# Rotary embedding on one core: cosine and sine tables loaded through ScalarE's queue instead of GpSimd's, and replicated without fill, shuffle or packing

## Chip, core and metric

One core of a Trainium2 chip. The metric is the device time of one execution in microseconds, the median of three runs. Engines are named as in the profile: DVE is VectorE, ACT is ScalarE, POOL is GpSimd, SP is SyncE; a trailing q means the engine's instruction queue. L96 is line 96 of the kernel before.

## What is computed

`x` has 16 batches of 512 positions with 16 heads of 64 floats. Half of each head is rotated, the other half passes through. The tables `cos` and `sin` have 512 rows of 32 floats, of which only the first 16 are used.

```python
x1, x2 = x[..., :32], x[..., 32:]
c, s = cos[None, :, None, :16], sin[None, :, None, :16]
first  = x1[..., :16] * c - x1[..., 16:] * s
second = x1[..., :16] * s + x1[..., 16:] * c
out = concatenate([first, second, x2], -1)
```

The input of x and the output are 33.55 MB each; each table is 64 KB.

## The kernel before

The flattened input is cut into T = 4 tiles of 128 partitions; a partition holds K = 16 successive positions of 16 heads, 64 KB in one piece. A ring of NS = 3 tiles lies in SBUF. A tile is loaded whole, rotated in place and stored whole, the half x2 travelling along untouched.

Tile 2 is loaded in two halves, since only the first half is wanted early. SyncE's queue carries, in this order: load 0, load 1, the first half of load 2 (lines 65 to 67); then, behind a wait for the rotation of tile 0, store 0, the second half of load 2, and load 3 (which takes the ring slot of tile 0 and so waits for store 0 to have landed); then store 1 and store 3. Store 2 is issued from POOL's queue (line 116). A dependency put in by hand (lines 118 to 123) holds store 1 until the second piece of tile 2 has been rotated.

`rotate` (lines 90 to 103) does one piece of a tile on VectorE in four instructions: x1 times sine into a PSUM tile (L96), x1 times cosine in place (L97), a subtraction for the first quarter (L98) and an addition for the second (L101). The pieces are half tiles, except that the second half of tile 2 is cut in 5 and 3 positions.

Because 512 positions are 32 partitions of 16, partition p of every tile needs table row p modulo 32. The lines before the first rotation build `table`, which holds for all 128 partitions and 16 positions the 16 cosines twice and the 16 sines twice, so that one multiply covers both quarters:

- L61: VectorE fills the first quarters of `stage` with zeros.
- L62 to 64: POOL's queue loads the 32 rows of each table (2 KB a row) to every fourth partition of `stage`, one transfer for the cosines and one for the sines. Both wait for L61.
- L73: a shuffle within each group of 32 partitions brings the eight filled rows of that group to the right places of `spun`.
- L80: four copies, of 32, 24, 16 and 8 partitions, put the rows of the four groups together on partitions 0 to 31 (`packed`).
- L83: four copies of 32 partitions and 1024 elements write `packed` to the four groups of `table`, doubling each row by reading it twice.

The order of work is that of the program text on each engine's queue; semaphores are placed by the tile framework from the data dependencies.

Of the kernel before, what the change touches and what calls it, by code (L numbers as in the profile page):

```python
# [1 line left out]

# [4 lines left out]


@with_exitstack
def kernel(  # L10
    ctx: ExitStack,
    tc: tile.TileContext,
    x: bass.AP,
    cos: bass.AP,
    sin: bass.AP,
    out: bass.AP,
):
    nc = tc.nc
    fp32 = mybir.dt.float32
    P = 128  # L20
    B, S, H, D = x.shape
    Q = D // 4
    HF = D // 2

    K = 16
    T = B * S // (P * K)
    PB = S // K
    REP = P // PB  # L30
    R = H * D
    NS = 3
    KC = K // 2
    KM = 13

    xf = x.rearrange("b s h d -> (b s h d)").rearrange("(t p f) -> t p f", t=T, p=P)
    of = out.rearrange("b s h d -> (b s h d)").rearrange("(t p f) -> t p f", t=T, p=P)
    cosf = cos.rearrange("(p k) j -> p (k j)", k=K)
    sinf = sin.rearrange("(p k) j -> p (k j)", k=K)

    const_pool = ctx.enter_context(tc.tile_pool(name="const", bufs=1))
    b_pool = ctx.enter_context(tc.tile_pool(name="bp", bufs=1, space=bass.MemoryType.PSUM))


    ring = const_pool.tile([P, NS, K, H, D], fp32)
    stage = const_pool.tile([P, 2, K, HF], fp32)
    spun = const_pool.tile([P, 2 * K, Q], fp32)
    packed = const_pool.tile([PB, 2 * K, Q], fp32)
    table = const_pool.tile([P, 2, K, 2, Q], fp32)

    def rows(t, lo, hi):
        return ring[:, t % NS, lo:hi].rearrange("p k h d -> p (k h d)")

    def load(t, lo=0, hi=K):
        return nc.sync.dma_start(out=rows(t, lo, hi), in_=xf[t, :, lo * R : hi * R])

    def store(t, lo=0, hi=K, queue=nc.sync):
        return queue.dma_start(out=of[t, :, lo * R : hi * R], in_=rows(t, lo, hi))  # L58


    nc.vector.memset(stage[:, :, :, 0:Q], 0.0)  # L61
    spread = stage.rearrange("(j b) t k i -> j b t (k i)", b=REP)  # L62
    nc.gpsimd.dma_start(out=spread[:, 0, 0], in_=cosf)  # L63
    nc.gpsimd.dma_start(out=spread[:, 0, 1], in_=sinf)  # L64
    load(0)
    load(1)
    load(2, 0, KC)

    PQ = PB // REP
    nc.vector.stream_shuffle(  # L73
        out=spun[:],
        in_=stage.rearrange("p t k j -> p (t k) j")[:, :, 0:Q],
        mask=[j % PQ * REP for j in range(PB)],
    )
    for q in reversed(range(REP)):
        n = PQ * (q + 1)
        nc.vector.tensor_copy(out=packed[0:n], in_=spun[q * PB : q * PB + n])  # L80

    for r in range(REP):
        nc.vector.tensor_copy(  # L83
            out=table[r * PB : (r + 1) * PB].rearrange("p t k c j -> p (t k) c j"),
            in_=packed.unsqueeze(2).to_broadcast((PB, 2 * K, 2, Q)),
        )
    C = table[:, 0].rearrange("p k c j -> p k (c j)")
    Sn = table[:, 1].rearrange("p k c j -> p k (c j)")

    def rotate(t, lo, hi):  # L90
        x1 = ring[:, t % NS, lo:hi, :, 0:HF]
        c = C[:, lo:hi].unsqueeze(2).to_broadcast((P, hi - lo, H, HF))
        s = Sn[:, lo:hi].unsqueeze(2).to_broadcast((P, hi - lo, H, HF))
        b_full = b_pool.tile([P, KC, H, HF], fp32, name="b_t")
        b_t = b_full[:, 0 : hi - lo]
        nc.vector.tensor_mul(out=b_t, in0=x1, in1=s)  # L96
        nc.vector.tensor_mul(out=x1, in0=x1, in1=c)  # L97
        nc.vector.tensor_sub(  # L98
            out=x1[:, :, :, 0:Q], in0=x1[:, :, :, 0:Q], in1=b_t[:, :, :, Q:HF]
        )  # L100
        return nc.vector.tensor_add(  # L101
            out=x1[:, :, :, Q:HF], in0=x1[:, :, :, Q:HF], in1=b_t[:, :, :, 0:Q]
        )

    rotate(0, 0, KC)
    rotate(0, KC, K)
    store(0)
    load(2, KC, K)
    load(3)
    rotate(1, 0, KC)  # L110
    rotate(1, KC, K)
    behind_loads = store(1)
    rotate(2, 0, KC)
    near = rotate(2, KC, KM)
    rotate(2, KM, K)
    store(2, queue=nc.gpsimd)

    tc.add_manual_dep(
        behind_loads.ins,
        near.ins.name,  # L120
        mybir.DependencyInfo(mybir.DependencyClass.Sync, mybir.DependencyReason.DATA),
        reason="the store follows the loads at the DMA engines",
    )
    rotate(3, 0, KC)
    rotate(3, KC, K)
    store(3)


# [1 line left out]
_INS = ['x', 'cos', 'sin']  # L130
_OUTS = [((16, 512, 16, 64), 'float32')]


# [23 lines left out]
```

## Time and profile before

| | |
|---|---|
| three runs | 161.46, 161.57, 162.91 us; median 161.57 |
| profiled execution | span from first to last instruction 159.5 us; its own time outside the profiler is not given |
| VectorE busy | 112.9 us (71% of the span), 47 instructions |
| POOL busy | 1.9 us, 7 instructions |
| ScalarE, TensorE | no work |
| bytes moved | 67.24 MB, 422 GB/s over the span |
| HBM read, written | 33.69 MB, 33.55 MB |
| cosine transfer, issue to landing | 8.9 us |
| sine transfer, issue to landing | 13.3 us |
| VectorE's longest wait | 14.4 us, at the shuffle, for the sine transfer |

A profile row of section 5 of the page names line, engine, operation, tiles and shapes, then total busy time and the mean of one instruction, then the idle time ahead of it and what ended that. DMA shares are those of 16 transfer engines; the queue called q1 holds the transfers issued from SyncE, q0 those from POOL. "Packet records" in the text are the trace's single entries for each packet on each transfer engine, with start, duration and size.

### The profile page before, as it was taken

The page shows a single profiled execution, that of the slowest core. Times are in us where ns is not written, and L with a number is a line of the kernel's source. Part 1 is how long each engine was busy: PE and PEld are TensorE (multiplying, and loading weights), DVE is VectorE, ACT ScalarE, POOL GpSimd, SP SyncE. Part 2 cuts the span into 40 slices and gives each one's busy share as a digit, 9 for nine tenths or more (in the row PEclk, how much of TensorE's full clock was granted, in tenths as well). Part 3 has the DMA queues.
Part 4 walks back from the last instruction along what each step waited for, and adds up shares of the span by engine and source line. Part 5 has one row for each costly group of instructions (what it writes and reads, how often), then busy time and mean ns, then how long its engine had stood idle before and what let it go on. Part 6 is the DMA issues. An engine that isn't in the chain of part 4 may idle for free.

```text
span 159.5 us, 115 instructions
## 1 busy us (share of the span) xinstructions
DVE 112.9 (71%) x47; POOL 1.9 (1%) x7
## 2 busy tenths in 40 slices
DVE  1000959999999999999999999999999990000000
POOL 3000000000000000000000000010000000000000
DMA  7969979899699699699996996996996996998966
GB/s 263 542 263 542 444 345 526 362 427 526 271 493 551 263 526 526 263 395 427 493 526 263 526 526 263 526 526 263 526 526 263 526 510 279 526 427 362 526 263 263
DMA packets 1360, 67.24 MB, mean 422 GB/s; under 512 B 176, under 2 KB 176, under 8 KB 208
## 3 DMA queue, kind: packets, MB, share of 16 engines
q1 hardware_dynamic: 1152, 58.72, 85.7%
q0 software_dynamic: 208, 8.52, 12.4%
HBM read 33.69 MB, written 33.55 MB: 422 GB/s over the span
## 4 chain that ended last, share of the span: by engine, by line
DVE 61%; DMA 14%; issue 5%; DVEq 1%
DVE b_t L96 22%; DVE ring L97 22%; DMA ring<-in_x_dram 14%; DVE ring L101 10%; DVE ring L98 7%; DVEq L152 1%; DVEq L96 0%
## 5 line engine op out<-in xcount | busy, mean ns | idle before, releaser
L96 DVE TENSOR_TENSOR b_t<-ring,table 128x4096 f32<-128x4096 f32 (+2 forms) x9 | 35.6, 3959 | 2.1 <-DMA ring<-in_x_dram 1.9
L97 DVE TENSOR_TENSOR ring<-ring,table 128x4096 f32<-128x4096 f32 (+2 forms) x9 | 35.6, 3950 | 0.3
L98 DVE TENSOR_TENSOR ring<-ring,b_t 128x2048 f32<-128x2048 f32 (+2 forms) x9 | 18.4, 2050 | 0.3
L101 DVE TENSOR_TENSOR ring<-ring,b_t 128x2048 f32<-128x2048 f32 (+2 forms) x9 | 18.4, 2043 | 0.0
L73 DVE LOAD_MASK_SELECT spun<-stage x1 | 0.0, 14 | 14.4 <-DMA stage<-in_sin_dram 14.4
L83 DVE COPY table<-packed 32x1024 f32<-32x1024 f32 x4 | 2.7, 684 | 0.1
L58 POOL DMA_DIRECT2D out_dram<-ring x1 | 0.6, 559 | 101.7 <-DVE ring L101 101.7
L80 DVE COPY packed<-spun 32x512 f32<-32x512 f32 (+3 forms) x4 | 1.7, 416 | 0.1
L61 DVE MEMSET stage<- 128x512 f32 x1 | 0.5, 485 | 0.9 <-PEq L141 0.9
L73 DVE STREAM_SHUFFLE spun<-stage 128x512 f32<-128x512 f32 x1 | 0.7, 722 | 0.0
L63 POOL DMA_DIRECT2D stage<-in_cos_dram x1 | 0.6, 642 | 1.3 <-DVE stage L61 1.3
L64 POOL DMA_DIRECT2D stage<-in_sin_dram x1 | 0.5, 532 | 0.0
L141 POOL MEMSET const-bfloat16-1.0<- 128x1 bf16 x1 | 0.1, 101 | 0.0
L141 POOL MEMSET const-float32-0.0<- 128x1 f32 x1 | 0.1, 98 | 0.2 <-issue 0.2
L141 POOL MEMSET const-float32-1.0<- 128x1 f32 x1 | 0.1, 98 | 0.0
L141 POOL MEMSET const-uint8-127<- 128x1 uint8 x1 | 0.1, 98 | 0.0
## 6 DMA issues: line engine op xcount, KB each, us to landing
ring<-in_x_dram SPq DMA_DIRECT2D x2, 4096.0 KB, 40.7
stage<-in_cos_dram POOLq DMA_DIRECT2D x1, 64.0 KB, 8.9
stage<-in_sin_dram POOLq DMA_DIRECT2D x1, 64.0 KB, 13.3
ring<-in_x_dram SPq DMA_DIRECT2D x3, 28.9
out_dram<-ring SPq DMA_DIRECT2D x3, 27.4
out_dram<-ring POOLq DMA_DIRECT2D x1, 39.5
```

The source lines that it names most:

```text
L58: return queue.dma_start(out=of[t, :, lo * R : hi * R], in_=rows(t, lo, hi))
L61: nc.vector.memset(stage[:, :, :, 0:Q], 0.0)
L63: nc.gpsimd.dma_start(out=spread[:, 0, 0], in_=cosf)
L64: nc.gpsimd.dma_start(out=spread[:, 0, 1], in_=sinf)
L73: nc.vector.stream_shuffle(out=spun[:], in_=stage.rearrange("p t k j -> p (t k) j")[:, :, 0:Q], mask=[j % PQ * REP for j in range(PB)],)
L80: nc.vector.tensor_copy(out=packed[0:n], in_=spun[q * PB : q * PB + n])
L83: nc.vector.tensor_copy(out=table[r * PB : (r + 1) * PB].rearrange("p t k c j -> p (t k) c j"), in_=packed.unsqueeze(2).to_broadcast((PB, ...
L96: nc.vector.tensor_mul(out=b_t, in0=x1, in1=s)
L97: nc.vector.tensor_mul(out=x1, in0=x1, in1=c)
L98: nc.vector.tensor_sub(out=x1[:, :, :, 0:Q], in0=x1[:, :, :, 0:Q], in1=b_t[:, :, :, Q:HF])
L101: return nc.vector.tensor_add(out=x1[:, :, :, Q:HF], in0=x1[:, :, :, Q:HF], in1=b_t[:, :, :, 0:Q])
L152: with _tile.TileContext(nc) as tc:
```

## The change

The tables go straight to the partitions where the replicating copies read them: the cosines to partitions 0 to 31 of `packed`, the sines to partitions 64 to 95, through two transfers on ScalarE's queue which wait for nothing. The fill, the shuffle, the packing copies and the tiles `stage` and `spun` are gone. Instead of four copies that write cosines and sines together there are eight, four for the cosines and then four for the sines, each of 32 partitions and 512 written elements. In the changed kernel's instruction lists SyncE and POOL keep their x and output transfers in the same order, and VectorE goes from ten instructions ahead of the first multiply (memset, shuffle, eight copies; the mask load of the shuffle not counted) to eight copies. The first cosine copy waits for the cosine transfer, the first sine copy for the sine transfer, and the first multiply for load 0 and the copies.

```diff
+    OS = 64
...
-    stage = const_pool.tile([P, 2, K, HF], fp32)
-    spun = const_pool.tile([P, 2 * K, Q], fp32)
-    packed = const_pool.tile([PB, 2 * K, Q], fp32)
+    packed = const_pool.tile([2 * OS, K, HF], fp32)
     table = const_pool.tile([P, 2, K, 2, Q], fp32)
...
-    nc.vector.memset(stage[:, :, :, 0:Q], 0.0)
-    spread = stage.rearrange("(j b) t k i -> j b t (k i)", b=REP)
-    nc.gpsimd.dma_start(out=spread[:, 0, 0], in_=cosf)
-    nc.gpsimd.dma_start(out=spread[:, 0, 1], in_=sinf)
+    nc.scalar.dma_start(out=packed[0:PB].rearrange("p k j -> p (k j)"), in_=cosf)
+    nc.scalar.dma_start(out=packed[OS : OS + PB].rearrange("p k j -> p (k j)"), in_=sinf)
     load(0)
     load(1)
     load(2, 0, KC)
...
-    PQ = PB // REP
-    nc.vector.stream_shuffle(
-        out=spun[:],
-        in_=stage.rearrange("p t k j -> p (t k) j")[:, :, 0:Q],
-        mask=[j % PQ * REP for j in range(PB)],
-    )
-    for q in reversed(range(REP)):
-        n = PQ * (q + 1)
-        nc.vector.tensor_copy(out=packed[0:n], in_=spun[q * PB : q * PB + n])
-
-    for r in range(REP):
-        nc.vector.tensor_copy(
-            out=table[r * PB : (r + 1) * PB].rearrange("p t k c j -> p (t k) c j"),
-            in_=packed.unsqueeze(2).to_broadcast((PB, 2 * K, 2, Q)),
-        )
+    for c, o in ((0, 0), (1, OS)):
+        for r in range(REP):
+            nc.vector.tensor_copy(
+                out=table[r * PB : (r + 1) * PB, c],
+                in_=packed[o : o + PB, :, 0:Q].unsqueeze(2).to_broadcast((PB, K, 2, Q)),
+            )
```

## The prediction

> **What bounds the kernel now.** I read the DMA queues first, since the page's busy table gives VectorE only 71%, then busy shares by stretch, then the chain of work, then the timeline of the first 23 us where every changed line lies.
>
> DMA queues, on the page: kind, packets, MB, share of 16 engines' span.
>
> ```profile
> q1 hardware_dynamic: 1152, 58.72, 85.7%
> q0 software_dynamic: 208, 8.52, 12.4%
> ```
>
> Together 98.1% of the span. What is left over is found in the busy table by stretch (stretch, its length, VectorE, POOL, clock, DMA share, GB/s):
>
> ```profile
> 0.00:1.70 1.70, 0.48 (x1) 0.20 (x4) 1.00 0.00 0
> 1.70:22.90 21.20, 5.13 (x10) 1.17 (x2) 1.00 1.08 451
> 22.90:51.00 28.10, 27.80 (x9) 0.00 (x0) 1.00 0.95 410
> 51.00:71.00 20.00, 19.86 (x6) 0.00 (x0) 1.00 1.02 434
> 71.00:99.80 28.80, 28.52 (x12) 0.00 (x0) 1.00 0.99 427
> 99.80:131.20 31.40, 31.09 (x12) 0.56 (x1) 1.00 1.00 434
> 131.20:158.20 27.00, 0.00 (x0) 0.00 (x0) 1.00 0.99 427
> 158.20:159.50 1.30, 0.00 (x0) 0.00 (x0) 1.00 0.00 0
> ```
>
> The transfer engines work from 1.7 to 158.2 us and never pause (shares around 1.00 scatter because whole packets are booked at a boundary). The packet records behind this view say the same: on each of the 16 engines no gap above 34 ns. A 64 KB packet takes 2.418 us there, and 8 tiles in and out are 64 such packets per engine: 154.8 us. So the end is bytes over DMA rate, plus 1.7 us before the first packet, about 0.9 us that the very first packet takes longer (3.284 against 2.418 us), the tables, and 1.3 us after the last one. Time can be won only in these margins; it is lost wherever the engines run dry.
>
> The chain of work (start, length, what) shows what could run them dry:
>
> ```profile
> 0.74 22.16 DMA ring<-in_x_dram
> 22.89 0.03 issue
> 22.92 0.02 DVEq L96
> 22.94 0.04 issue
> 22.99 4.44 DVE b_t L96
> ```
>
> It goes from the landing of the first tile straight into the first multiply; the table work isn't in it. From 22.99 us VectorE runs without a gap and its ends time the stores: the first store is issued at 49.87 us, and the packet records end the loads queued ahead of it at 51.02 on the earliest engine. Issue to first packet took 1.0 us on this queue (0.74 to 1.74 us for the first load). So 50.87 against 51.02: 0.15 us of slack. A start of the rotation that is late by d costs about d - 0.15, and since the engines have no later pause, nothing gives it back.
>
> The timeline of the start (start, length, engine, line, what, and in brackets idle before it and its releaser):
>
> ```profile
> 0.74 1.33 SPq L55 DMA_DIRECT2D ring<-in_x_dram  x3
> 0.92 0.48 DVE L61 MEMSET stage<- 128x512 f32 x1 [0.92 <-PEq L141]
> 1.70 0.64 POOL L63 DMA_DIRECT2D stage<-in_cos_dram  x1 [1.26 <-DVE stage L61]
> 2.34 0.53 POOL L64 DMA_DIRECT2D stage<-in_sin_dram  x1
> 15.80 0.72 DVE L73 STREAM_SHUFFLE spun<-stage 128x512 f32<-128x512 f32 x1
> 16.56 1.77 DVE L80 COPY packed<-spun 32x512 f32<-32x512 f32 x4
> 18.36 2.78 DVE L83 COPY table<-packed 32x1024 f32<-32x1024 f32 x4
> 22.99 4.43 DVE L96 TENSOR_TENSOR b_t<-ring,table 128x4096 f32<-128x4096 f32 x1 [1.85 <-DMA ring<-in_x_dram]
> ```
>
> The table is complete at 18.36 + 2.78 = 21.14 us and VectorE then idles 1.85 us for the tile. That is the cover of the whole table path.
>
> **The change part by part.** *Fill, shuffle, packing gone.* Removed from VectorE: memset 0.485, mask load 0.014, shuffle 0.722, four packing copies 4 x 0.416, four wide copies 4 x 0.684: 5.62 us. Added: eight copies of 32x512. That size has a row, the packing copies (416 ns, also 32 partitions and 512 elements): 8 x 0.416 = 3.33 us. VectorE falls from 112.9 to 110.6 us. Nothing of these 2.3 us reaches the end: all of it lies before 22.99 us, in time that ends on the tile's landing.
>
> *Transfers moved from POOL to ScalarE.* POOL loses issues of 0.642 and 0.532 us and its wait for the memset (1.26 us). ScalarE, with no work before, gets two issues (nearest row: SyncE's load, 0.424 us each) and nothing stands behind them. SyncE's eight transfers keep their order; its loads no longer compete with earlier software transfers, which weren't late. POOL's third transfer, the store of tile 2, becomes the first software transfer of the program. It waits for VectorE until 104.58 us as before; its first packet came at 109.5 us. SyncE's store of tile 1 fills the engines from 99.85 for 19.3 us, so a first software transfer slower by up to 9 us still leaves no gap: cost 0.
>
> *Table packets.* Before, each engine carried two 4 KB packets (two rows each) of 0.159 us, 0.32 us in all. The page's shares agree: 8.39 MB of q0 at q1's rate make 12.24% of its 12.4%, leaving 0.1 to 0.2%, some 0.2 to 0.3 us. The bytes stay the same. Bounds for the new cost: below, 0 (hidden in the long first packet); above, four packets per engine (one per row) that each pay the first packet's excess, 4 x 0.87 = 3.5 us. I take 0.32, the row of the same bytes on the same engines.
>
> [...]
>
> *When the tables are ready.* In the records an engine serving both queues alternates packet by packet: table data at 7.2 us, its semaphore write at 9.8, the second table at 12.2 and 14.8, spacing 2.5 us. ScalarE should issue close to SyncE's 0.74 us, so its packets miss at most the first slot, and the next opens at 5.3 us on the last engine. With one packet per row a table takes three slots (two rows, semaphore), both take six: the sine's semaphore at 5.3 + 5 x 2.5 = 17.8, seen by VectorE 0.48 us later (15.30 to 15.78 before), four sine copies 1.72 us with their gaps: ready at 20.0, the cosine copies being done by then. Packets of two rows: four slots, ready at 15.0. Either is before 22.99.
>
> *Sum.* Tile landing 22.99 + 0, engines' work + 0, ends + 0: span 159.5. The three times shown are 161.46, 161.57 and 162.91; the page gives a span only, so 2.07 us lie around it to the median, and I leave them. Forecast 161.5.
>
> **Rivals.** *Table slots overrun (slower).* The place is the alternation in the first tile's load. From four slots per table the sine's semaphore comes at 5.3 + 7 x 2.5 = 22.8, the table at 25.0, VectorE starts 2.0 late, minus 0.15: 163.4. If 32 rows go to four engines, eight rows each plus a semaphore, the 18th slot is at 47.8, table 50.0, + 27: 188.5. For it: no record shows small rows on a hardware queue, and each big row is its own packet there. Against it: big loads spread evenly over 16 engines, and two rows each need only six slots. It decides from eight slots up.
>
> *Tables behind the loads (slower).* If SyncE's and ScalarE's transfers share something that is served in order, the tables wait for tile 0: both at about 22.9, eight copies 3.4 and 0.5 to be seen, start near 26.8: + 3.7, 165.2. If the sines wait for tile 1 (semaphores end at 41.86 us), start 44.4, + 21: 183. For it: SyncE hands over three loads within 1.33 us, long before they move. Against: in the trace the software queue overtook them.
>
> [...]
>
> *Dearer table packets:* the upper bound above, + 0.5 to + 3.1, up to 164.7; nothing in the trace resembles it once engines are running.
>
> *Faster:* table packets hide in the first packet's excess: at most 0.32 + 0.87 = 1.2 us, 160.4. Over 1% (1.62 us) isn't reachable from there; the first issue at 0.74 follows the start barrier in either kernel. That the change doesn't do what it says would look like the forecast.
>
> **How the numbers follow.** Forecast 0.70 (own range 160.8 to 162.5), overrun 0.13, behind the loads 0.07, dearer packets 0.05, faster 0.05. A measurement tells about 1% from no change: 159.95 to 163.2. Faster than that: 0.03, part of the last case and errors outside the list. Slower: 0.13 + 0.07 + most of the dearer case = 0.24. Same: 0.73. The range 160.6 to 164.7 leaves out the severe overruns (about half of 0.13), the tables behind loads (0.07) and 0.02 below: 0.16.
>
> **What the changed profile would show.** Right: the hardware queues hold all but one transfer; VectorE busy 110.6 us; eight copies of about 416 ns, the last ending between 15 and 20 us; the first multiply again released by the tile's landing, near 23 us; DMA share 1.0 from 1.7 to 158. Wrong: the first multiply follows directly on a copy, or copies wait for the sines past 20.8 us; a stretch near 51 us with DMA share clearly under 1; a first packet of the loads later than 1.74 us.

## The result, and the profile after

The changed kernel takes 163.60 us (median of six runs, 163.24 to 164.69) against 161.56 before: ratio 1.0125, 95% interval 1.0092 to 1.0158, so about 2.0 us slower. The six runs of before lie between 161.46 and 162.91. The profiled execution of the changed kernel took 163.8 us itself and has a span of 161.6, 2.1 more than before; what lies around the span (2.2 us) is as it was.

The table path did nearly what was forecast. Timeline of the changed kernel's start (start, length, engine, line, what, idle before and its releaser):

```profile
0.74 0.40 ACTq L60 DMA_DIRECT2D packed<-in_cos_dram  x1
0.74 1.33 SPq L54 DMA_DIRECT2D ring<-in_x_dram  x3
1.17 0.45 ACTq L61 DMA_DIRECT2D packed<-in_sin_dram  x1
11.01 1.71 DVE L71 COPY table<-packed 32x512 f32<-32x512 f32 x4 [11.01 <-DMA packed<-in_cos_dram]
18.69 1.71 DVE L71 COPY table<-packed 32x512 f32<-32x512 f32 x4 [5.97 <-DMA packed<-in_sin_dram]
23.62 4.43 DVE L84 TENSOR_TENSOR b_t<-ring,table 128x4096 f32<-128x4096 f32 x1 [3.21 <-DMA ring<-in_x_dram]
```

The table is finished at 20.40 us and VectorE waits another 3.21 us for the tile. So the tables aren't late; the tile is. The chain of work names the same step as before, grown from 22.16 to 22.77 us:

```profile
0.74 22.77 DMA ring<-in_x_dram
23.52 0.03 issue
23.57 0.05 issue
23.62 4.44 DVE b_t L84
```

The DMA queues of the changed kernel show the tables on a queue of their own, q10, with 96 packets where POOL's queue needed 64 (32 for rows, 32 semaphore writes):

```profile
q1 hardware_dynamic: 1152, 58.72, 85.1%
q0 software_dynamic: 144, 8.39, 12.0%
q10 hardware_dynamic: 96, 0.13, 0.2%
```

Busy by stretch, to be held against the same stretches before (columns as there):

```profile
1.70:22.90 21.20, 3.34 (x8) 0.00 (x0) 1.00 1.07 442
22.90:51.00 28.10, 27.18 (x9) 0.00 (x0) 1.00 0.97 417
51.00:71.00 20.00, 19.86 (x6) 0.00 (x0) 1.00 1.01 419
71.00:99.80 28.80, 28.52 (x12) 0.00 (x0) 1.00 1.02 437
```

The busy share stays at 1.0. The bytes don't show the loss either: fewer pass in the first stretch (442 GB/s, before 451) and the third (419, before 434), but more in the second (417, before 410) and the fourth (437, before 427), and over 1.7 to 99.8 us both kernels come to 429 GB/s. A packet is booked whole where it starts (hence shares over 1, such as 1.07), so a loss of this size gets lost in the boundaries. A share of 1.0 says that packets are under way, not that they move at full rate on every engine.

The packet records show it. Where the last of the 16 engines writes its semaphore at the end of each transfer (us):

| end of | before | after | lost by then |
|---|---|---|---|
| load of tile 0 | 22.54 | 23.00 | 0.46 |
| load of the first half of tile 2 | 51.54 | 52.07 | 0.53 |
| store of tile 0 | 71.25 | 72.13 | 0.88 |
| load of the second half of tile 2 | 80.94 | 82.70 | 1.76 |
| load of tile 3 | 100.25 | 102.35 | 2.10 |
| store of tile 3 | 158.21 | 160.31 | 2.10 |

So the loss has three parts: 0.46 us while the tables load, about 0.4 at the end of store 0, and about 1.2 by one engine that falls behind after it. Of that last part: at the end of the second half of tile 2 the median engine is at 81.67, the last at 82.70; before, 80.66 and 80.94. Its first packet there starts at 72.40 us, the last of all, and takes 1.80 us instead of 1.21. It didn't start late because its part of store 0 was late: the last semaphore for store 0 was written at 72.13 us. Pairing each engine's semaphore with the packet that starts as it ends leaves three semaphores (71.63, 71.73, 71.85 us) and three later starts (71.82, 72.12, 72.40); by this pairing the engine carried nothing for at least 0.54 us. Summed over the 16 engines the idle time at this change is 1.06 us; before there is none.

### The profile page after: what moved, and what is told of

Read it like the earlier page. It is cut to its first block, busy times and chain, and to the rows that moved or that the text cites. A ratio compares the mean times of both kernels' runs of the same rounds, so it can differ in the third digit from the quotient of the medians.

```text
span 161.6 us, 110 instructions
## 1 busy us (share of the span) xinstructions
DVE 110.6 (68%) x44; POOL 0.9 (1%) x5
## 4 chain that ended last, share of the span: by engine, by line
DVE 61%; DMA 14%; issue 5%; DVEq 1%
DVE b_t L84 22%; DVE ring L85 22%; DMA ring<-in_x_dram 14%; DVE ring L89 10%; DVE ring L86 7%; DVEq L140 1%; DVEq L84 0%
## 5 line engine op out<-in xcount | busy, mean ns | idle before, releaser
L71 DVE COPY table<-packed 32x512 f32<-32x512 f32 x8 | 3.3, 418 | 17.1 <-DMA packed<-in_cos_dram 11.0
```

The source lines that it names most:

```text
L71: nc.vector.tensor_copy(out=table[r * PB : (r + 1) * PB, c], in_=packed[o : o + PB, :, 0:Q].unsqueeze(2).to_broadcast((PB, K, 2, Q)),)
```

## The experiments

Four theories were held at first. Q: the tables' new queue. L: their new destination, or the tiles that moved with it. S: store 2 being the first transfer that POOL issues. R: ScalarE and SyncE issuing at the same moment.

One measure from the packet records is used throughout: how much longer packets took than 2.418 us (64 KB), 1.213 (32 KB), 0.159 (4 KB) or 0.084 (2 KB), summed over a stretch and divided by 16 engines. For e18 and e19, which have other sizes too, 1.519 (40 KB) and 0.916 (24 KB) are added. A second measure is the idle time between store 0 and the load behind it: the starts of the 16 engines' next packets less the ends of their semaphore writes, summed over the engines. The sum doesn't depend on which packet belongs to which engine.

| run | longer at 5 to 30 us | longer at 66 to 78 us | idle between store 0 and the next load, sum of 16 engines | last engine behind the median, end of second half of tile 2 | median time, us |
|---|---|---|---|---|---|
| before | 0.01 | 0.38 | 0.0 | 0.28 | 161.56 |
| after | 0.38 | 0.89 | 1.06 | 1.03 | 163.60 |
| e1 old layout, ScalarE | 0.00 | 0.79 | 0.20 | 0.30 | 164.72 |
| e2 new layout, POOL | 0.50 | 0.95 | 0.40 | 1.01 | 163.85 |
| e4 tables twice | 0.76 | 0.66 | 0.83 | 1.09 | 163.94 |
| e5 no tables | 0.01 | 0.24 | 0.0 | 0.24 | 160.93 |
| e6 after, tile 0 in halves | 0.36 | 0.02 | 0.0 | 0.31 | 162.73 |
| e7 before, tile 0 in halves | 0.00 | 0.00 | 0.0 | 0.44 | 162.67 |
| e8 before, 0.3 us late | 0.00 | 0.62 | 0.0 | 0.23 | 161.60 |
| e9 before, 0.4 us late | 0.00 | 0.77 | 0.0 | 0.33 | 161.86 |
| e10 before, extra pair on 32 neighbours | 0.39 | 0.90 | 0.0 | 0.18 | 165.02 |
| e11 before, extra pair on every fourth | 0.00 | 0.88 | 0.11 | 0.21 | 164.82 |
| e12 before, extra pair on every second | 0.38 | 0.80 | 0.0 | 0.25 | 165.00 |
| e13 after, tiles back | 0.40 | 0.98 | 1.09 | 1.60 | 163.64 |
| e14 before, extra pair crowded | 0.51 | 1.12 | 1.27 | 1.29 | 163.91 |
| e15 before, extra pair spread | 0.00 | 0.38 | 0.0 | 0.25 | 163.01 |
| e16 after, store 0 early | 0.26 | 0.07 | 0.0 | 0.26 | 162.08 |
| e17 before, store 0 early | 0.00 | 0.05 | 0.0 | 0.58 | 161.71 |
| e18 after, longer loads | 0.56 | 0.05 | 0.0 | 0.54 | 162.50 |
| e19 before, longer loads | 0.00 | 0.00 | 0.0 | 0.33 | 162.35 |

The columns of packets and of idle time come from one profiled execution each, the last column from four to ten runs.

### Queue or destination

e1, the old destination on the new queue:

```diff
-    nc.gpsimd.dma_start(out=spread[:, 0, 0], in_=cosf)
-    nc.gpsimd.dma_start(out=spread[:, 0, 1], in_=sinf)
+    nc.scalar.dma_start(out=spread[:, 0, 0], in_=cosf)
+    nc.scalar.dma_start(out=spread[:, 0, 1], in_=sinf)
```

> The kernel before, with only the queue of its two table transfers changed from POOL to ScalarE; fill, shuffle and packing stay, and the transfers still wait for the fill. Theory Q (the loss of about 2 us comes from the tables riding on a hardware queue, one row per packet, whatever the destination): 163.2 to 163.8. Theory L (the loss comes from the new destination, 32 neighbouring partitions, or from the moved tiles): 161.6. Theory S (the loss comes from store 2 being the program's first software transfer): 163.2 to 163.8, as under Q. If the loss needs ScalarE and SyncE to issue at the same moment (theory R, the race at the start), 161.6 to 162.1, since here ScalarE issues near 1.5 us.

e2, the new destination on the old queue:

```diff
-    nc.scalar.dma_start(out=packed[0:PB]...
-    nc.scalar.dma_start(out=packed[OS : OS + PB]...
+    nc.gpsimd.dma_start(out=packed[0:PB]...
+    nc.gpsimd.dma_start(out=packed[OS : OS + PB]...
```

> The changed kernel with its two table transfers put back on POOL's queue, issued at once; destination, eight copies and missing fill stay. Theory Q, S and R: 161.5, the whole loss gone. Theory L: 163.2 to 163.8, the loss stays.

Measured: e1 164.72 us (ratio 1.0201, 1.0183 to 1.0218), above every forecast; e2 163.85 (1.0149, 1.0101 to 1.0197). Theories Q, S and R fall with e2: the loss stays on POOL's queue. e1 loses for another reason, which its timeline shows:

```profile
20.70 0.72 DVE L73 STREAM_SHUFFLE spun<-stage 128x512 f32<-128x512 f32 x1
21.46 1.76 DVE L80 COPY packed<-spun 32x512 f32<-32x512 f32 x4
23.25 2.77 DVE L83 COPY table<-packed 32x1024 f32<-32x1024 f32 x4
26.06 4.43 DVE L96 TENSOR_TENSOR b_t<-ring,table 128x4096 f32<-128x4096 f32 x1
```

Here the first multiply follows directly on a copy: the sines came at 20.2 us (six slots, starting one later, as ScalarE waited for the fill and issued at 1.43 us instead of 0.74) and the long conversion made the table late. The rotation starts 3.07 us later than before and the span is 3.1 us longer: the first rival of the prediction, run by accident in another kernel, at about its price (d - 0.15 would be 2.9). And while its rows load, no packet is longer (0.00), nor does an engine fall behind. So the small packets of a hardware queue by themselves don't cost what the changed kernel lost.

### How many packets, and none at all

e4 and e5, on the changed kernel:

```diff
+    nc.scalar.dma_start(out=again[0:PB]...
+    nc.scalar.dma_start(out=again[OS : OS + PB]...
```

> The changed kernel with both table transfers issued a second time on ScalarE's queue, into a tile that nothing reads: four more row packets per engine. If each row packet costs about 0.19 us of engine time (0.084 of its own and 0.1 on the 64 KB packet behind it, as in the changed kernel's records), the loads of tile 0 land 0.75 us later and the total rises by 0.75 to about 164.4. If a row packet costs only its own 0.084 us, + 0.35: 164.0. If a disturbance later in the kernel grows with the number of row packets as well, over 165. Under S or L the number of packets matters by their own time only: 164.0.

```diff
-    nc.scalar.dma_start(out=packed[0:PB]...
-    nc.scalar.dma_start(out=packed[OS : OS + PB]...
...
+    nc.vector.memset(table[:], 0.5)
```

> The changed kernel without any table transfer: the table is filled with a constant by VectorE, so cosines and sines are left out of the result. Store 2 remains POOL's, now the first software transfer. Theory Q and R: 161.2 (the 161.5 of before less 0.3 us of table packets). Theory S: 162.7 to 163.4, since the late spread of the engines would stay. Theory L: 161.2.

Measured: e4 163.94 us (1.0157, 1.0129 to 1.0185), e5 160.93 (0.9965, 0.9955 to 0.9974). In e4 the lengthening doubles (0.76 after 0.38) and tile 0 lands 0.3 us later, but the total rises by 0.3 only, inside the scatter of the two. The profiled execution, the slowest of its four at 164.54, is 0.7 above the changed kernel's, so the times don't decide between the 164.0 and the 164.4 of the forecast; the packets speak for the latter. e5 puts the price of all tables in the kernel before at 0.66 us. Store 2 being the first transfer from POOL costs nothing there: S is out a second time.

### Is it the hand-over from loads to store 0?

Theory H: in the changed kernel store 0 is issued 1.01 us ahead of the end of the loads (50.50 against 51.51), before 1.15 (49.87 against 51.02). Perhaps those 0.15 us cost 1.6. The issues of store 0, before and in the changed kernel:

```profile
49.87 0.35 SPq L58 DMA_DIRECT2D out_dram<-ring  x1
```

```profile
50.50 0.35 SPq L57 DMA_DIRECT2D out_dram<-ring  x1
```

e6 on the changed kernel, e7 on the kernel before, the same edit:

```diff
-    load(0)
+    load(0, 0, KC)
+    load(0, KC, K)
```

> The changed kernel with tile 0 loaded in two halves, so that VectorE starts on the first half and store 0 is issued some 10 us ahead of the end of the loads instead of 1.0 us. Theory H (about 1.6 of the 2.1 us come from the hand-over: store 0 is issued 1.0 us before the loads end, where it was 1.15, and the price appears around 68 to 82 us, at the change from store 0 to the next load; the other 0.45 us come from the new destination slowing the loads of tile 0): 161.4 to 162.0, packets at 68 to 75 us without the long ones. Theory P (the new destination puts the 16 engines into another phase, which makes the later change from store to load dearer whatever the issue time): 162.8 to 163.6, the long packets stay.

> The kernel before with the same two halves of tile 0. Theory H: the slack of store 0 grows from 1.15 to over 10 us, and the 0.2 to 0.9 us by which packets near 68 us are longer shrinks as well: 160.8 to 161.3. Theory P: 161.6, no change but for the halves.

e8 (64 elements) and e9 (512), on the kernel before:

```diff
+    late = stage.rearrange("p t k i -> p (t k i)")[:, 0 : 1 * D]
+    nc.vector.tensor_copy(out=late, in_=ring[:, 0, 0, 0:1].rearrange("p h d -> p (h d)"))
     rotate(0, 0, KC)
```

> The kernel before with one small copy from tile 0 (128 x 64) on VectorE ahead of the first multiply, which nothing else needs: the rotation starts about 0.2 us later, store 0 is issued about 0.95 us before the loads end. The tables' way is untouched. Theory H: over proportion, 162.2 to 163.2, with longer packets near 68 to 72 us as in the changed kernel. Theory P: 161.6 to 161.8, the delay less the slack of 0.15.

> The same with a copy of 128 x 512: the rotation starts about 0.45 us later, store 0 is issued about 0.7 us before the loads end. Theory H: 162.7 to 163.6. Theory P: 161.9, the delay less the slack of 0.15.

Measured: e8 161.60 us (1.0009, 0.9985 to 1.0033), e9 161.86 (1.0021, 1.0000 to 1.0042); e6 162.73 (1.0065, 1.0044 to 1.0086), e7 162.67 (1.0062, 1.0041 to 1.0084). Theory H falls: store 0 is issued 0.94 and 0.82 us ahead of the loads' end in e8 and e9, later than in the changed kernel, and costs no more than the lateness. Their packets at 66 to 78 us are longer by 0.62 and 0.77, almost as much as in the changed kernel, yet no engine goes idle or falls behind: longer packets at this place aren't the loss by themselves. But theory P misses e6 as well: with store 0 queued long ahead, the changed kernel loses 0.9 us of its loss and the long packets at 66 to 78 us are gone (0.02), while the same halves make the kernel before slower by 1.1, which neither theory forecast. There the packets are longer by 1.11 us per engine at 30 to 51 us, all of them the last ones of the load ahead of store 0. So in the kernel before the price moves from the end of store 0 to its beginning; in the changed kernel 0.29 us of it is found there. In halves, both kernels take the same time.

### Which property of the destination

In e10 to e12 a second pair of table transfers was added on POOL's queue, into a tile that nothing reads: `again[0:32]` and `again[64:96]` in e10, every fourth partition in e11, every second one (0 to 62, 64 to 126) in e12. e13 puts 6 KB of padding ahead of `table` in the changed kernel.

> The kernel before, plus one more pair of table transfers on POOL's queue behind its own, into a tile that nothing reads, on partitions 0 to 31 and 64 to 95 as in the changed kernel. The tables in use, their way, and the issue time of store 0 stay. Theory D (the new destination costs twice: 0.45 us while it is written, and about 1 us on one engine that falls behind at 72 to 82 us): 162.8 to 163.6, with 64 KB packets behind the extra rows at 2.5 to 2.7 us. Theory M (only the 0.45 us belong to the destination, and the engine that falls behind belongs to the moved tiles or to the tight hand-over): 162.2 to 162.5.

> The same extra pair, into every fourth partition as the kernel before loads its own. Both theories: only the engines' own time of two packets of 0.159 us, 161.9, no 64 KB packet over 2.45 us behind the extra rows and no engine left behind.

> The same extra pair, into every second partition: 0 to 62 for the one, 64 to 126 for the other, so not neighbours, but again one half of the partitions for each transfer. If what counts is that each transfer's rows crowd into one half of the partitions: as with neighbours, 162.2 or more, packets behind the rows at 2.5 to 2.7 us. If what counts is that the partitions are neighbours: 161.9, as every fourth.

> The changed kernel with 6 KB of unused space in each partition ahead of the finished table, so that this tile lies where it lay before; nothing else. Theory D: no change, 163.2 to 163.8, one engine about 1 us behind at the end. Theory A (the moved table disturbs the transfers at 68 to 82 us by its address): the engine that falls behind is gone, 162.1 to 162.5.

Measured: 165.02, 164.82 and 165.00 us; e13 163.64 (1.0145, 1.0111 to 1.0179). The three times say little, since one extra transfer came to stand ahead of the tables in POOL's queue and the tables were late, as e10's timeline shows:

```profile
1.27 0.64 POOL L66 DMA_DIRECT2D again<-in_cos_dram  x1 [0.82 <-PEq L155]
1.90 0.55 POOL L64 DMA_DIRECT2D stage<-in_cos_dram  x1
26.46 4.43 DVE L99 TENSOR_TENSOR b_t<-ring,table 128x4096 f32<-128x4096 f32 x1
```

Their packets still answer the question. At 5 to 30 us they are longer by 0.39 us per engine in e10 and by 0.38 in e12, by 0.00 in e11. The longer packets of e10 and e12 start right behind the extra rows (32 in each run, 2.57 us in the median), and none behind the spread rows of the tables in use, which the same queue carries between them. It isn't direct neighbours that count: rows of one transfer which all lie in one half of the partitions cost extra, rows spread over all 128 don't. With the half goes the step from row to row, 1 or 2 partitions in e10 and e12 and 4 in e11; which of the two counts is not shown. The same three runs show something else: in e10 and e12, crowded as they are, no engine falls behind (0.18 and 0.25, in e11 0.21). There store 0 is issued only after the loads have ended, since the tables are late (in e10 at 53.35 us, the first engine ending its loads at 51.89). So theory D fails in e10 as to the engine that falls behind. e13 rules out the address of the moved table: one engine stays behind.

e14 and e15 repeat the pair behind the tables, crowded and spread (a third page of `stage`, and the fill grown with it):

```diff
+    nc.gpsimd.dma_start(out=stage[0:32, 2]..., in_=cosf)      # e14
+    nc.gpsimd.dma_start(out=stage[64:96, 2]..., in_=sinf)
...
+    nc.gpsimd.dma_start(out=spread[:, 0, 2], in_=cosf)        # e15
+    nc.gpsimd.dma_start(out=spread[:, 1, 2], in_=sinf)
```

> The kernel before, plus one more pair of table transfers to partitions 0 to 31 and 64 to 95 of a page that nothing reads, this time issued behind the tables in use (the earlier try put one of the extra transfers ahead of them, and the tables came 5 us later). Theory D (crowding the rows on half of the partitions costs 0.4 us then, and later leaves one engine about 1 us behind at 72 to 82 us): 162.9 to 163.6. Theory N (crowding costs only then; the engine that falls behind has another cause in the changed kernel): 162.1 to 162.5.

> The same extra pair behind the tables, to every fourth partition. Both theories: the own time of two packets, 0.32 us: 161.9, no engine left behind.

Measured: e14 163.91 us (1.0140, 1.0112 to 1.0168), e15 163.01 (1.0079, 1.0055 to 1.0103; ten runs from 161.85 to 163.84). Crowding brings into the kernel before all that the changed kernel showed: 0.51 us while it loads, 1.12 at 66 to 78 us, 1.27 us of idle engines between store 0 and the next load, one engine 1.29 behind. It came out 0.3 us above theory D's range. The rate of the engines at 67 to 82 us shows it in e14, and not in e15's profiled execution:

```profile
67.00:82.00 15.00, 14.90 (x5) 0.00 (x0) 1.00 0.90 358
```

```profile
67.00:82.00 15.00, 14.86 (x6) 0.00 (x0) 1.00 1.00 419
```

But e15 missed its forecast of 161.9 by 1.1 us. Its profiled execution took 161.85, its fastest, so what its slower ones do isn't recorded. One execution in ten of e8 (163.38) and of e9 (163.24) took as long, without crowded rows. Crowding is thus not the only way to such times; with it every execution of the changed kernel and of e14 took 163.2 us or more, and e14 is 0.9 us above e15.

### Giving store 0 room

e16 on the changed kernel and e17 on the kernel before:

```diff
-    rotate(0, KC, K)
+    rotate(0, KC, K - 1)
```

> The changed kernel with one of the 16 positions of tile 0 left unrotated, so that VectorE ends 1.7 us sooner on this tile and store 0 is issued some 2.7 us ahead of the end of the loads instead of 1.0. Theory B (an engine falls behind only where crowding at the start meets a pause between store 0 and the next load, and this pause comes from the late hand-over): 161.6 to 162.3, no engine behind at 82 us, no long packets near 68 us. Theory D (crowding alone suffices): 163.0 to 163.7.

> The kernel before with the same position left out, as the measure for the run above: store 0 issued 2.9 us ahead of the end of the loads. Theory B: the 0.37 us per engine by which packets near 68 us are longer go, 161.1 to 161.4. Theory D: 161.2 to 161.6.

e18 and e19, the same two kernels with all their work:

```diff
+    KL = 10
...
-    load(2, 0, KC)
+    load(2, 0, KL)
...
-    load(2, KC, K)
+    load(2, KL, K)
```

> The changed kernel, complete, with 10 instead of 8 positions of tile 2 in the load ahead of store 0 (and 6 in the one behind it): the loads end 2.4 us later, so store 0 is issued about 3.4 us ahead of their end. Theory B (the larger part of the loss is a pause at a close hand-over from loads to store 0, which the crowded rows make dearer): 161.9 to 162.3, as with the position left out. Theory D: 163.0 to 163.7.

> The kernel before with the same 10 and 6 positions: 161.4 to 161.8 under both theories, 0.3 to 0.5 below the run above under theory B (the crowding alone).

Measured: e16 162.08 us (1.0033, 1.0022 to 1.0044), e17 161.71 (1.0010, 1.0000 to 1.0020); e18 162.50 (1.0055, 1.0040 to 1.0070), e19 162.35 (1.0042, 1.0027 to 1.0057). With room at the hand-over the changed kernel is 0.37 us behind its partner in the one pair and 0.15 in the other (there the intervals overlap), not 2.0. e16 met theory B's forecast and no engine goes idle in it or in e18. e17, e18 and e19 came out 0.2 to 0.6 us above theory B's. The profile's transfers, issue to landing in the median of the three whole-tile loads (which is load 3, the one issued when store 0 has landed), give the same answer; in the changed kernel:

```profile
ring<-in_x_dram SPq DMA_DIRECT2D x3, 30.2
```

and with store 0 early, e16:

```profile
ring<-in_x_dram SPq DMA_DIRECT2D x3, 28.7
```

In the kernel before it is this:

```profile
ring<-in_x_dram SPq DMA_DIRECT2D x3, 28.9
```

In e18 and e19 room wasn't free: the kernel before lost 0.7 us by it, with packets longer by 0.80 us per engine at 51 to 60 us, the last ones ahead of store 0. e18 has 0.02 there, and crowded rows at 0.56. So the 0.15 us between these two is no price of crowding; the partner lost its time elsewhere. And e17 didn't gain: its long packets at 66 to 78 us are gone (0.05), and 0.28 us per engine of longer ones stand at 30 to 66 us instead. None of the variants that do all the work beats the kernel before.

## Why the prediction was wrong

The wide range held the time, but the forecast of 161.5 was not the outcome: 163.6 is slower, by an amount that the likeliest case (160.8 to 162.5) excluded. That it lies in the wide range is in part luck: the range reached so far for an overrun of table slots, which didn't take place, and for dearer table packets, which hold a quarter of the loss. Of the signs named for being wrong none came, but for a first packet at 1.76 us instead of 1.74: the copies had their sines at 18.69 us, the first multiply follows the tile, and the busy share stays at 1.0.

- **The table path, as forecast.** Eight copies of 418 ns (forecast 416), VectorE busy 110.6 us, the sine's last semaphore write at 18.16 us (forecast 17.8), the table ready at 20.40 (20.0). Six slots, not eight: neither the overrun nor tables behind the loads took place. The packet records show ScalarE's and SyncE's packets in turn: q10's rows start 16 at a time, at 4.86 to 5.41, 7.35 to 7.92, 12.37 to 12.98 and 14.98 to 15.59 us, its semaphore writes at 9.95 to 10.52 and 17.60 to 18.16, and after each group of rows 16 packets of 64 KB on q1 follow (4.93 to 5.49 us after the first).
- **A start late by d costs d - 0.15: held roughly.** e1 is 3.07 late and 3.1 longer; e9 is 0.40 late and 0.26 longer; e8 is 0.30 late and no longer.
- **"I take 0.32" for the table packets failed in size.** The packets' own time was 4 x 0.084 = 0.34 us, as taken. But 64 KB packets behind three of the four crowded rows of each engine took 2.52 instead of 2.418 us: 0.38 us more per engine. With it "Tile landing 22.99 + 0" failed: the load's last semaphore came 0.46 us later and the first multiply started at 23.62. The row I took it from, two packets of 0.159, had its rows spread over all 128 partitions. I read size and engine from that row and not the destination, which the change altered. The rival of dearer packets had the sign and a chance of 0.05, with another cause.
- **"Engines' work + 0" failed, and it holds the larger part.** I took the stretch from 23 us on as fixed: bytes over rate, on engines that never pause. The records of before already showed that it isn't at full rate throughout: 0.38 us per engine of longer packets at 66 to 78 us, at the change from store 0 to the next load, which I had read over because the busy share there is 1.0 and the gaps are below 34 ns. In the changed kernel the packets there are longer by 0.89, engines do run dry (1.06 us summed over the 16, at least 0.54 of it on one), and one engine is left a microsecond behind. With room for store 0 (e16) the packets are longer by 0.07 and none is idle. About 1.6 of the 2.0 us are lost at this change.
- **What stays open.** Why an engine goes idle and falls behind, and how rows that landed before 20 us decide that at 72. Shown: not the queue (e2), not the table's address (e13), not a late store 0 alone (e8, e9); crowding does it (e14) where store 0 is issued about 1 us ahead of the end of the loads, and not where it has room (e16, e18) or comes after their end (e10, e12). e15 shows that even spread extra rows raise the time by more than their bytes: 1.4 us, against 0.32 for their packets. That the engines' relative timing carries it is only a guess: the records don't name the engine of a packet.

## What to carry to other kernels

Where transfers bound a kernel, compare when each transfer ends on its last engine, not the busy share: here the share was 1.0 in both, and the bytes up to 99.8 us were the same, while 2 us were lost in longer packets and one engine's pause. In this case small side loads were priced by where they land as well as by their bytes: rows spread over all partitions cost the packets behind them nothing (0.01 us per engine at most, crowded rows 0.38 in the changed kernel), which was worth a few copies on an idle engine. And a change between loading and storing is part of the schedule; what was done 50 us earlier made it dearer here (0.89 us per engine of longer packets, before 0.38), so an edit "hidden" at the start is measured at the end.

## What the runs showed of the hardware that was not expected

- Rows crowded on one half of the partitions lengthened the packets behind them on all engines, by 0.26 to 0.56 us per engine for two tables of 64 KB (least in e16, most in e18; after 0.38); rows on every fourth partition by 0.01 at most (before, e1, e11). Whether the half or the small step between rows counts is not shown.
- The change from loads to store 0 and back cost between 0.1 (e18) and 1.2 us (e14) per engine in longer packets: mostly in the last packets of the store where it was issued about 1 us ahead (0.38 before), and in the last packets of the load ahead of it in e7 (1.11) and e19 (0.80), where it was queued long ahead.
- At that change single engines went idle, 0.4 to 1.3 us summed over the 16, in the five runs with crowded rows and a store issued 0.7 to 1.2 us ahead of the loads' end (after, e2, e4, e13, e14); 0.20 at most in the others.
- Without its tables, 0.2% of the bytes, the kernel gets 0.35% faster (e5).
- ScalarE's hardware queue moved one row of 2 KB per packet (after: 64 packets, 0.084 us each), POOL's queue two rows (before: 32 packets of 4 KB, 0.159 us each).
